# A decoder step on one core: another order of the last down projection and its norm, and sample states loaded three ahead

## The chip, the core and the metric

The kernel runs on one core of a Trainium2 chip. The metric is device time in microseconds, the median of several runs. The engines that matter are TensorE (PE, matmuls), VectorE (DVE), ScalarE (ACT), GpSimd (POOL, here mostly an issuer of DMAs) and SyncE (SP, an issuer of DMAs). Each engine works through its own instructions in order and waits on semaphores for the others.

## The reference, cut to what matters

One layer of a hybrid decoder for 512 prompt tokens and 8 samples with one token each: a half-step SwiGLU feed-forward network, a mixer (pooling and a state space model), a second feed-forward network, and a last RMS norm. The change touches the second feed-forward network, the last norm, and the new states of the samples.

```python
h = h + 0.5 * _swiglu(_rms_norm(h, ffn1_norm), ...)      # D_MODEL 1024, FFN_DIM 2816
h = h + mixer(_rms_norm(h, mix_norm))
h = h + 0.5 * _swiglu(_rms_norm(h, ffn2_norm), ...)
y = _rms_norm(h, final_norm)
# new state of one sample, per head: decay * old state + (dt * x) outer B
h_new = exp(dt * A) * h0 + (dt * x)[:, None] * B[None, :]
```

## The kernel before, in words

The features lie on the 128 partitions and the 520 tokens (512 and 8) along the free dimension, in two halves of 260 (`HALVES`, `HB`). `h` holds 8 feature tiles of 520 tokens. Weights are float32; each is split into a rounded part (`whi`, cast by ACT, L107) and a rest (`wlo`, DVE, L108), and each product is three matmuls (`mm3`, L117 to L119).

The second feed-forward network works in three chunks of 8, 8 and 6 of its 22 hidden tiles. For each chunk, gate and up products are computed (PSUM tiles `A` and `BE`), and then the down projection adds the chunk to `h`. The weights of `w2gu` and `w2d` come in loads issued by SP into two raw pairs of buffers; a load is issued when DVE has read the pair that it overwrites.

**Down stages of the first two chunks** (`down`, L350): for each of 8 output tiles `d`, the weights are loaded and split, PE runs 48 matmuls into `dn`, and DVE adds the result to `h` (`td`, L367, then L371). Into these two stages the new states of the samples are woven: the generator `new_states` (L806) yields 16 steps, one for each sample and head group, and `STATES` (L37) says how many are taken ahead of each output tile. A step works on one tile `hs` of 128x4x128: POOL issues the loads of the row `br` (broadcast to all partitions) and of the old state `hs`; ACT scales `br` into a tile `so`, four times; DVE multiplies `hs` by the decay and adds `so`, four times; POOL issues the store `out_nss`. The loads run two steps ahead, in three buffers. All these DMAs stand in POOL's one queue of instructions, a load behind the store whose buffer it needs.

**Last chunk** (`down_by_half`, L392): all first halves of the tokens (b = 0) come first, then all second halves (b = 1), so that the norm of the first half runs beside the second half's matmuls. The accumulators `dh` are banks of 512 floats: two neighbouring output tiles share one tile of two banks (`BE`), others take single banks (`A`). Except for what is pinned with `keep_in_program_order`, a scheduler that simulates times orders the instructions at build time; in the program that it makes, PE takes up the output tiles out of their order and in pieces (2, 0, 3, 4, 6, 7 among others). `done` (L419) scales the accumulator (`th`, L422), adds it to `h` (L424) and calls `after2`, which sums the squares (`sumsq`, L141) into `last` and multiplies by the gain into `hg`.

**Norm** (`finish`, L540): one matmul with ones sums the squares over partitions (`psl`, L543; for the last output tile a second one, L545), ACT takes the square root, and DVE, in two quarters of 130 tokens, takes the reciprocal, multiplies four feature tiles at a time, and SP stores each piece of 4 tiles by 130 tokens.

Of the kernel before, what the change touches and what calls it, by code (L numbers as in the profile page):

```python
# [9 lines left out]
F32 = mybir.dt.float32  # L10
F32R = mybir.dt.float32r
AF = mybir.ActivationFunctionType
ALU = mybir.AluOpType
# [3 lines left out]
P = 128  # L17
D = 1024
# [3 lines left out]
HB = NT // 2  # L22
HALVES = (slice(0, HB), slice(HB, NT))
KD = D // P
# [9 lines left out]
CHUNKS = (8, 8, 6)  # L34
NG = 9
ON_ACT = 4
STATES = (0, 1, 1, 1, 2, 1, 1, 1)  # L37

CONV_PLAN = (
    "b0 b1 d0 b2 b3 x0 x1 v0 d1 x2 x3 d2 X0 p0 y0 c0 A0 p1 x4 m0 x5 B0 c1 p2 m1 A1 x6 c2 p3 A2 B1 x7 "  # L40
# [22 lines left out]
def tile_trunk_step(ctx: ExitStack, tc: tile.TileContext, ins: dict, outs: dict):  # L63
    nc = tc.nc
# [7 lines left out]
    tmp = ctx.enter_context(tc.tile_pool(name="tmp", bufs=3, side="right"))  # L72
    dr = ctx.enter_context(tc.tile_pool(name="dr", bufs=1, space=DRAM))
    ps = [None]
# [6 lines left out]
    h = vx[:, NVEC:].rearrange("p (d t) -> p d t", d=KD)  # L81
# [4 lines left out]
    ones = cst.tile([P, P], F32, tag="ones", name="ones")  # L86
    nc.vector.memset(ones, 1.0)
    eps = cst.tile([P, 1], F32, tag="eps", name="eps")
# [24 lines left out]
        nc.sync.dma_start(out=raw, in_=src)  # L113
        return split(raw, n, name, wp, 3, ("whi", "wlo"))

    def mm3(ps, whi, wlo, xhi, xlo, start, stop, **kw):
        nc.tensor.matmul(ps, whi, xhi, start=start, stop=False, **kw)  # L117
        nc.tensor.matmul(ps, whi, xlo, start=False, stop=False, **kw)  # L118
        nc.tensor.matmul(ps, wlo, xhi, start=False, stop=stop, **kw)  # L119

    def ws(w, k, m=P):
        return w[:, k * m : (k + 1) * m]
# [18 lines left out]
    def sumsq(acc, d, hs, name):  # L141
        n = hs.stop - hs.start
        if d == 0:
            nc.scalar.activation(out=acc[:, hs], in_=h[:, d, hs], func=AF.Square)
        else:
            sq = tmp.tile([P, HB], F32, tag="ta", name=f"sq_{name}_{d}")
            nc.scalar.activation(out=sq[:, :n], in_=h[:, d, hs], func=AF.Square)
            nc.vector.tensor_tensor(out=acc[:, hs], in0=acc[:, hs], in1=sq[:, :n], op=ALU.add)
# [47 lines left out]
    class Ffn:  # L196
# [195 lines left out]
        def down_by_half(self, c, lo, after, wd):  # L392
            n = KF - lo
            banks, units = {}, []
            for d in range(KD):
                src, name = ins[f"w{self.i}d"][d, :, lo * P :], f"{self.i}d{d}_{c}"
                raw = raw_tile(name)[:, : n * P]
                nc.sync.dma_start(out=raw, in_=src)
                if d < 4:
                    home = (wp, 3, ("whi", "wlo")) if d < 2 else (self.wx, 2, ("shi", "slo"))  # L400
                    units.append(split(raw, n * P, name, *home))
                    continue
                hi, lw = (wd.tile([P, n * P], F32R, tag=t, bufs=KD - 4, name=f"{t}_{name}") for t in ("dhi", "dlo"))
                nc.scalar.copy(hi, raw)
                nc.vector.tensor_tensor(out=lw, in0=raw, in1=hi.bitcast(F32), op=ALU.subtract)
                units.append((hi, lw))

            def part(d, b, ks):
                if (d, b) not in banks and d % 4 < 2:
                    t = ps[0].tile([P, 2, 512], F32, tag="BE", bufs=2, name=f"dh{self.i}_{d}{b}")  # L410
                    banks[d, b], banks[d + 1, b] = t[:, 0], t[:, 1]
                elif (d, b) not in banks:
                    banks[d, b] = ps[0].tile([P, 512], F32, tag="A", bufs=2, name=f"dh{self.i}_{d}{b}")
                wh, wl = units[d]
                for k in ks:
                    g = self.g[lo + k]
                    mm3(banks[d, b][:, :HB], ws(wh, k), ws(wl, k), g[:, 0, b], g[:, 1, b], k == 0, k == n - 1)

            def done(d, b):  # L419
                hs = HALVES[b]  # L420
                t = self.wx.tile([P, 2, HB], F32, tag="tg", bufs=2, name=f"th{self.i}_{d}{b}")[:, 0]
                nc.vector.scalar_tensor_tensor(out=t, in0=banks[d, b][:, :HB], scalar=-0.5, in1=self.nx[3][:, hs],  # L422
                                               op0=ALU.mult, op1=ALU.mult)
                nc.vector.tensor_tensor(out=h[:, d, hs], in0=t, in1=h[:, d, hs], op=ALU.add)  # L424
                after(d, b, hs)

            for d in range(3):
                part(d, 0, range(n - 1))
            for b in range(2):
                for d in range(KD):  # L430
                    part(d, b, range(n - 1, n) if b == 0 and d < 3 else range(n))
                    done(d, b)
# [10 lines left out]
    for j in range(KD // 2):  # L443
        for d in (j, j + KD // 2):
            q = slice(NVEC + d * NT if d else 0, NVEC + (d + 1) * NT)
# [70 lines left out]
    last = act.tile([P, NT], F32, tag="acc", name="acc_last")  # L516
    res = []

    def before2():
# [3 lines left out]
        res.append(f2["hg"].tile([P, NT], F32, tag="rl", name="r_last"))  # L523
        return f2["hg"]

    def after2(d, b, hs):
        hg = res[0]
        if (d, b) == (KD - 1, 1):
            sq = tmp.tile([P, HB], F32, tag="ta", name="sq_last")
            nc.scalar.activation(out=sq, in_=h[:, d, hs], func=AF.Square)  # L530
            nc.vector.tensor_scalar(out=hg[:, d, hs], in0=h[:, d, hs], scalar1=v("final_norm", d), scalar2=None,
                                    op0=ALU.mult)
            finish(1, sq)
            return
        sumsq(last, d, hs, f"l{d}{b}")
        nc.scalar.activation(out=hg[:, d, hs], in_=h[:, d, hs], func=AF.Copy, scale=v("final_norm", d))
        if (d, b) == (KD - 1, 0):
            finish(0)

    def finish(b, sq=None):  # L540
        hs, hg, rl = HALVES[b], *res
        ps = bank(f"psl{b}")
        nc.tensor.matmul(ps[:, :HB], ones, last[:, hs], start=True, stop=sq is None)  # L543
        if sq is not None:
            nc.tensor.matmul(ps[:, :HB], ones, sq, start=False, stop=True)  # L545
        nc.scalar.activation(out=rl[:, hs], in_=ps[:, :HB], func=AF.Sqrt, bias=eps, scale=1.0 / D)
        cuts = (hs.start, hs.start + HB // 2, hs.stop)
        for t in (slice(cuts[0], cuts[1]), slice(cuts[1], cuts[2])):
            n = t.stop - t.start
            tc.keep_in_program_order(nc.vector.reciprocal(out=rl[:, t], in_=rl[:, t]))  # L550
            for q in (slice(0, 4), slice(4, KD)):
                nc.vector.tensor_tensor(out=hg[:, q, t], in0=hg[:, q, t],
                                        in1=rl[:, t].unsqueeze(1).to_broadcast([P, 4, n]), op=ALU.mult)
                nc.sync.dma_start(out=outs["y"][:, q, t], in_=hg[:, q, t])

    f2["ffn"].rest(before2, after2)
    for p in (ps[0], f2["st"], g2, f2["hg"], f2["wx"]):
# [3 lines left out]
def mixer(tc, ins, outs, e):  # L561
    nc = tc.nc
    cst, act, wp, tmp, dr, pool = (e[x] for x in ("cst", "act", "wp", "tmp", "dr", "pool"))
    ones = e["ones"]
    bank, load_unit, mm3, ws, v, rstd, rstds, vec, h, nx2, raw_tile, open_f2, fin, fill = (
        e[x] for x in ("bank", "load_unit", "mm3", "ws", "v", "rstd", "rstds", "vec", "h", "nx2", "raw_tile",
                       "open_f2", "fin", "fill"))
    xh, xl, _, r = nx2[0]
# [183 lines left out]
    sdec = cst.tile([P, NX, NS], F32, tag="sdec", name="sdec")  # L752
# [52 lines left out]

    def new_states(wx):  # L806
        def load(b, g):
            br = wx.tile([P, P], F32, tag="sb", bufs=3, name=f"br{b}{g}")
            tc.keep_in_program_order(nc.gpsimd.dma_start(out=br, in_=rows_bc(b, 0, g)))
            hs = wx.tile([P, 4, P], F32, tag="sh", bufs=3, name=f"hs{b}{g}")  # L810
            tc.keep_in_program_order(nc.gpsimd.dma_start(out=hs, in_=ins["state_ssm"][:, b, 4 * g : 4 * g + 4]))
            return br, hs

        todo = [(b, g) for g in range(2) for b in range(NS)]
        ahead = [load(*todo[0]), load(*todo[1])]
        for i, (b, g) in enumerate(todo):
            yield
            br, hs = ahead.pop(0)
            if i + 2 < len(todo):
                ahead.append(load(*todo[i + 2]))  # L820
            o = wx.tile([P, 4, P], F32, tag="so", bufs=2, name=f"so{b}{g}")
            for q in range(4):
                j = 4 * g + q
                tc.keep_in_program_order(
                    nc.scalar.activation(out=o[:, q], in_=br, func=AF.Copy, scale=sxdt[:, j, b : b + 1]))
                tc.keep_in_program_order(
                    nc.vector.scalar_tensor_tensor(out=hs[:, q], in0=hs[:, q], scalar=sdec[:, j, b : b + 1],
                                                   in1=o[:, q], op0=ALU.mult, op1=ALU.add))
            tc.keep_in_program_order(nc.gpsimd.dma_start(out=outs["nss"][:, b, 4 * g : 4 * g + 4], in_=hs))
        yield  # L830

# [268 lines left out]
```

## Time and profile before

| | |
|---|---|
| median of 3 runs | 1002.59 us (1002.44 to 1002.99) |
| profiled execution | 1003.51 us, its span 1000.5 us |
| granted TensorE clock | 0.994 (mean) |
| busy: PE, DVE, ACT, POOL | 97%, 81%, 53%, 9% of the span |
| chain that ended last | PE 88%, DVE 6%, ACT 2%, POOL 2% |
| stores of `y` (8) | 260 KB each, median 3.5 us from issue to landing |
| state loads and stores (16 each) | 256 KB each, median 3.6 and 3.1 us |

Times within the profile are microseconds from the start of the span. In a row of the timeline the first number is the start, the second the time until the end of the last of the instructions in the row, and in brackets stands how long the engine was idle before it and for whom it waited. "x4" counts instructions. A DMA's row on POOL or SP is the time to issue it, not the transfer.

### The profile page before, as it was taken

The numbers are of one execution on the slowest core, as the hardware profiler recorded it, in microseconds if no ns is written. First come the engines' busy times: TensorE is split into PE (matmuls) and PEld (weight loads), VectorE is DVE, ScalarE is ACT, GpSimd is POOL, SyncE is SP. The second block draws the span as 40 slices with busy tenths as digits, with TensorE's granted clock in tenths as the row PEclk, the third lists the DMA queues.
The fourth block names the chain that finished last, engine by engine and source line by source line (L and its number), as shares of the span: only waits on it lengthen the run. The fifth ranks groups of instructions, "written<-read, shape, count | busy, mean of one in ns | idle before, by whom it ended". The sixth has DMA issues, their size and how long they took to land.

```text
span 1000.5 us, 19362 instructions
## 1 busy us (share of the span) xinstructions
PE 971.7 (97%) x7850; PEld 951.4 (95%) x7850; DVE 806.9 (81%) x1408; ACT 528.7 (53%) x881; POOL 87.8 (9%) x157
## 2 busy tenths in 40 slices
PE   7999999999999999999999999999999999999994
PEld 6899999999999999999899998899999999999993
DVE  7999657996569688788979987999957999668865
ACT  7566414664145455684845235666743666436552
POOL 0000000000000000167312000100012000120000
PEclk9999999999999999999999999999999999999997
DMA  6333232323223223263334421423346333452213
GB/s 194 112 126 114 98 101 73 124 88 124 85 85 106 85 104 117 87 216 105 107 133 122 146 90 54 124 94 118 127 137 187 120 127 118 124 195 96 95 33 85
DMA packets 44072, 114.44 MB, mean 114 GB/s; under 512 B 6408, under 2 KB 15560, under 8 KB 43984
## 3 DMA queue, kind: packets, MB, share of 16 engines
q1 hardware_dynamic: 40912, 103.78, 30.7%
q0 software_dynamic: 3072, 9.44, 3.5%
q8 instruction: 61, 1.00, 0.4%
q14 instruction: 27, 0.22, 0.1%
HBM read 105.86 MB, written 7.34 MB: 113 GB/s over the span
## 4 chain that ended last, share of the span: by engine, by line
PE 88%; DVE 6%; ACT 2%; POOL 2%; issue 1%; DMA 0%; SPq 0%; DVEq 0%; ACTq 0%
PE A L119 8%; PE A L117 8%; PE A L118 8%; PE dn L117 7%; PE dn L119 7%; PE dn L118 7%; PE BE L117 6%; PE BE L119 6%; PE BE L118 6%; PE P L232 4%; PE wo L117 2%; PE wo L118 2%; PE wo L119 2%; PE inz L117 2%; PE inz L119 2%; PE inz L118 2%
## 5 line engine op out<-in xcount | busy, mean ns | idle before, releaser
L117 PE MATMUL dn<-g,whi_1d 128*128 128x260 f32 x352 | 99.3, 283 | 0.2 <-DVE td L367 0.2
L118 PE MATMUL dn<-g,whi_1d 128*128 128x260 f32 x352 | 99.5, 283 | 0.0
L119 PE MATMUL dn<-g,wlo_1d 128*128 128x260 f32 x352 | 99.4, 283 | 0.0
L367 DVE SCALAR_TENSOR_TENSOR td<-dn,r_f 128x520 f32<-128x520 f32 x40 | 27.9, 699 | 73.2 <-PE dn L119 73.2
L119 PE MATMUL dn<-g,wlo_2d 128*128 128x260 f32 x256 | 72.4, 283 | 0.0
L118 PE MATMUL dn<-g,whi_2d 128*128 128x260 f32 x256 | 72.3, 282 | 0.0
L117 PE MATMUL dn<-g,whi_2d 128*128 128x260 f32 x256 | 72.3, 282 | 0.0
L117 PEld LDWEIGHTS dn<-g,whi_1d 128*128 128x128 f32 x352 | 66.1, 188 | 0.4 <-DVE td L367 0.4
L118 PEld LDWEIGHTS dn<-g,whi_1d 128*128 128x128 f32 x352 | 66.3, 188 | 0.0
L119 PEld LDWEIGHTS dn<-g,wlo_1d 128*128 128x128 f32 x352 | 66.2, 188 | 0.0
L297 ACT COPY ac<-A 128x260 f32<-128x260 f32 x123 | 45.6, 374 | 29.3 <-PE A L119 28.0
L107 ACT CAST whi_1d<-raw_1d 128x1024 fp32r<-128x1024 f32 (+1 forms) x24 | 23.4, 980 | 67.0 <-PE dn L118 54.2
L260 DVE TENSOR_TENSOR s<-raw 128x1024 f32<-128x1024 f32 x41 | 50.0, 1220 | 3.9 <-DMA raw<-in_w2gu 3.9
L232 PE MATMUL P<-xg_f,raw 128*128 128x260 f32 x192 | 45.1, 392 | 6.2 <-DMA raw<-in_w1gu 5.4
L232 PEld LDWEIGHTS P<-xg_f,raw 128*128 128x128 f32 x192 | 36.9, 195 | 12.1 <-ACT xg_f L179 5.4
L117 PEld LDWEIGHTS dn<-g,whi_2d 128*128 128x128 f32 x256 | 48.3, 189 | 0.0
L118 PEld LDWEIGHTS dn<-g,whi_2d 128*128 128x128 f32 x256 | 48.2, 188 | 0.0
L119 PEld LDWEIGHTS dn<-g,wlo_2d 128*128 128x128 f32 x256 | 48.2, 188 | 0.0
L118 PE MATMUL wo<-catg,whi_wo 128*128 128x260 f32 x128 | 36.4, 285 | 1.3 <-DVE catg L957 1.3
L117 PE MATMUL wo<-catg,whi_wo 128*128 128x260 f32 x128 | 37.3, 292 | 0.3 <-DVE h L926 0.3
L117 PE MATMUL inz<-xh_mx,whi_inz 128*128 128x260 f32 x128 | 36.8, 287 | 0.1
L117 PE MATMUL inx<-xh_mx,whi_inx 128*128 128x260 f32 x128 | 36.4, 284 | 0.0
(1340 smaller groups left out, 3924.1 us busy)
## 6 DMA issues: line engine op xcount, KB each, us to landing
raw<-in_w2gu SPq DMA_DIRECT2D x44, 512.0 KB, 4.5
raw<-in_w1gu SPq DMA_DIRECT2D x42, 512.0 KB, 4.4
raw_1d<-in_w1d SPq DMA_DIRECT2D x16, 512.0 KB, 4.4
raw_2d<-in_w2d SPq DMA_DIRECT2D x16, 512.0 KB, 4.6
raw_wo<-in_w_out SPq DMA_DIRECT2D x12, 512.0 KB, 5.0
ab<-scr_acs SPq DMA_DIRECT2D x8, 512.0 KB, 4.8
h<-in_state_ssm SPq DMA_DIRECT2D x16, 256.0 KB, 4.2
raw_inz<-in_w_in SPq DMA_DIRECT2D x8, 512.0 KB, 3.9
```

What stands on the lines that cost most here:

```text
L107: nc.scalar.copy(h, src)
L117: nc.tensor.matmul(ps, whi, xhi, start=start, stop=False, **kw)
L118: nc.tensor.matmul(ps, whi, xlo, start=False, stop=False, **kw)
L119: nc.tensor.matmul(ps, wlo, xhi, start=False, stop=stop, **kw)
L232: nc.tensor.matmul(self.banks[f, u][b][:, :HB], ws(self.raw[f][:, u], j + 4 * q), xg[:, slot[q]], start=j == q == 0, stop=j == 3 and q == ...
L260: nc.vector.tensor_tensor(out=s1, in0=diag, in1=up0, op=ALU.add)
L297: nc.scalar.copy(keep, out[:, :HB])
L367: nc.vector.scalar_tensor_tensor(out=t, in0=banks[d][:, :, :HB], scalar=-0.5, in1=self.nx[3].rearrange("p (b t) -> p b t", b=2), op0=ALU.mult,
```

## The change

The changed kernel does two things.

In the last chunk each output tile gets an accumulator bank of its own; the first matmul of each second-half tile (except output tile 1's) is pinned to the program order. The norm of the first half is started by the first tile of the second half and is spread over the tiles that follow: one reciprocal or one product with its store per tile. Products and stores cover 2 feature tiles by 260 tokens. In the second half the squares of the last two output tiles are kept apart and go to `psl` as matmuls of their own, three in all, and the square root is taken in two quarters.

For the states, loads run three steps ahead in four buffers. ACT multiplies the loaded state by the decay in place, and DVE adds the scaled row; the tile `so` is gone. `STATES` takes its first step ahead of output tile 2 and two steps ahead of tiles 3 and 5.

```diff
-STATES = (0, 1, 1, 1, 2, 1, 1, 1)
+STATES = (0, 0, 1, 2, 1, 2, 1, 1)
...
-    def mm3(ps, whi, wlo, xhi, xlo, start, stop, **kw):
-        nc.tensor.matmul(ps, whi, xhi, start=start, stop=False, **kw)
+    def mm3(ps, whi, wlo, xhi, xlo, start, stop, pin=False, **kw):
+        first = nc.tensor.matmul(ps, whi, xhi, start=start, stop=False, **kw)
+        if pin:
+            tc.keep_in_program_order(first)
...
-                if (d, b) not in banks and d % 4 < 2:
-                    t = ps[0].tile([P, 2, 512], F32, tag="BE", bufs=2, name=f"dh{self.i}_{d}{b}")
-                    banks[d, b], banks[d + 1, b] = t[:, 0], t[:, 1]
-                elif (d, b) not in banks:
-                    banks[d, b] = ps[0].tile([P, 512], F32, tag="A", bufs=2, name=f"dh{self.i}_{d}{b}")
+                if (d, b) not in banks:
+                    if b == 0 and d in (2, 3):
+                        banks[d, b] = bank(f"dh{self.i}_{d}{b}")
+                    elif d % 2:
+                        banks[d, b] = ps[0].tile([P, 512], F32, tag="A", bufs=2, name=f"dh{self.i}_{d}{b}")
+                    else:
+                        t = ps[0].tile([P, 2, 512], F32, tag="BE", bufs=2, name=f"dh{self.i}_{d}{b}")
+                        banks[d, b] = t[:, 0]
...
-                    mm3(banks[d, b][:, :HB], ws(wh, k), ws(wl, k), g[:, 0, b], g[:, 1, b], k == 0, k == n - 1)
+                    mm3(banks[d, b][:, :HB], ws(wh, k), ws(wl, k), g[:, 0, b], g[:, 1, b], k == 0, k == n - 1,
+                        pin=b == 1 and k == 0 and d != 1)
...
     def after2(d, b, hs):
         hg = res[0]
+        if (d, b) == (0, 1):
+            finish(0, [last[:, HALVES[0]]])
+        elif b and todo:
+            todo.pop(0)()
+        if b and d >= KD - 2:
+            late.append(tmp.tile([P, HB], F32, tag="ta", name=f"sq_last{d}"))
+            nc.scalar.activation(out=late[-1], in_=h[:, d, hs], func=AF.Square)
+        else:
+            sumsq(last, d, hs, f"l{d}{b}")
         if (d, b) == (KD - 1, 1):
...
-            finish(1, sq)
+            finish(1, [last[:, hs], *late])
+            while todo:
+                todo.pop(0)()
             return
...
+    def finish(b, sqs):
         hs, hg, rl = HALVES[b], *res
         ps = bank(f"psl{b}")
+        for k, sq in enumerate(sqs):
+            nc.tensor.matmul(ps[:, :HB], ones, sq, start=k == 0, stop=k == len(sqs) - 1)
+        cuts = (0, HB // 2, HB)
+        quarters = [slice(cuts[i], cuts[i + 1]) for i in range(2)]
+        for q in quarters:
+            nc.scalar.activation(out=rl[:, hs][:, q], in_=ps[:, q], func=AF.Sqrt, bias=eps, scale=1.0 / D)
+
+        def inverse(q):
+            tc.keep_in_program_order(nc.vector.reciprocal(out=rl[:, hs][:, q], in_=rl[:, hs][:, q]))
+
+        def out(d):
+            tc.keep_in_program_order(
+                nc.vector.tensor_tensor(out=hg[:, d : d + 2, hs], in0=hg[:, d : d + 2, hs],
+                                        in1=rl[:, hs].unsqueeze(1).to_broadcast([P, 2, HB]), op=ALU.mult))
+            nc.sync.dma_start(out=outs["y"][:, d : d + 2, hs], in_=hg[:, d : d + 2, hs])
+
+        todo.extend([lambda q=q: inverse(q) for q in quarters])
+        todo.extend([lambda d=d: out(d) for d in range(0, KD, 2)])
...
-            br = wx.tile([P, P], F32, tag="sb", bufs=3, name=f"br{b}{g}")
+            br = wx.tile([P, P], F32, tag="sb", bufs=4, name=f"br{b}{g}")
...
-            hs = wx.tile([P, 4, P], F32, tag="sh", bufs=3, name=f"hs{b}{g}")
+            hs = wx.tile([P, 4, P], F32, tag="sh", bufs=4, name=f"hs{b}{g}")
...
-        ahead = [load(*todo[0]), load(*todo[1])]
+        ahead = [load(*t) for t in todo[:3]]
...
-            if i + 2 < len(todo):
-                ahead.append(load(*todo[i + 2]))
-            o = wx.tile([P, 4, P], F32, tag="so", bufs=2, name=f"so{b}{g}")
+            if i + 3 < len(todo):
+                ahead.append(load(*todo[i + 3]))
...
-                    nc.scalar.activation(out=o[:, q], in_=br, func=AF.Copy, scale=sxdt[:, j, b : b + 1]))
+                    nc.scalar.activation(out=hs[:, q], in_=hs[:, q], func=AF.Copy, scale=sdec[:, j, b : b + 1]))
...
-                    nc.vector.scalar_tensor_tensor(out=hs[:, q], in0=hs[:, q], scalar=sdec[:, j, b : b + 1],
-                                                   in1=o[:, q], op0=ALU.mult, op1=ALU.add))
+                    nc.vector.scalar_tensor_tensor(out=hs[:, q], in0=br, scalar=sxdt[:, j, b : b + 1], in1=hs[:, q],
+                                                   op0=ALU.mult, op1=ALU.add))
```

## The prediction

> **What bounds the kernel now.** I read the page first: TensorE is busy 97% of the span, and 88% of the chain that ended last is PE. So an edit is worth something only where PE stops, or after PE has ended. From PE's start times in the timeline from 640 us on (pitch 0.12 us per 128x260 matmul) I then listed each place where the next matmul came late. Between 657.5 and 958.7 us there is none above 0.07 us. The whole stage in which the sample states are written lies in there, so its waits are covered today. Losses begin at 958.67 us, with the last matmuls. The chain in order of time shows them (start, us, engine, tile, line):
>
> ```profile
> 958.99 0.44 DVE th L422
> 959.47 0.39 PE dh L117
> ...
> 979.91 0.35 DVE th L422
> 980.30 0.39 PE dh L117
> 984.91 0.77 DVE th L422 x2
> ...
> 987.28 0.44 DVE acc_last L148
> 987.76 1.14 PE psl L543 x2
> 988.90 0.88 PE psl L545 x2
> 989.81 0.49 ACT r_last L546
> ```
>
> Twice PE waits for `th` to read a PSUM bank that it shares with another accumulator, and after the last matmul (start 984.60) a row of DVE and ACT steps runs before the sum of squares `psl`. PE's own timeline gives these waits, in brackets:
>
> ```profile
> 959.47 0.39 PE L117 MATMUL dh<-g,whi_2d 128*128 128x260 f32 x1 [0.52 <-DVE th L422]
> 980.30 0.39 PE L117 MATMUL dh<-g,dhi_2d 128*128 128x260 f32 x1 [0.73 <-DVE th L422]
> 987.76 1.14 PE L543 MATMUL psl<-acc_last,ones 128*128 128x260 f32 x2 [2.89 <-DVE acc_last L148]
> ```
>
> Behind that, the stores. In stretches of 1 us (engines, clock, DMA share, GB/s), the first-half store at 978 and the last ones:
>
> ```profile
> 978.00:979.00 1.00, 1.00 (x11) 1.00 (x10) 1.00 (x4) 0.55 (x2) 0.00 (x0) 1.00 1.01 290
> 993.00:994.00 1.00, 0.00 (x0) 0.00 (x0) 0.96 (x2) 0.00 (x0) 0.00 (x0) 0.50 0.97 279
> 997.00:998.00 1.00, 0.00 (x0) 0.00 (x0) 0.00 (x0) 0.00 (x0) 0.00 (x0) 0.50 0.96 166
> ```
>
> 1.06 MB takes from 993.0 to 998.1 us, and the clock has fallen to 0.50 while PE stood. For the states, POOL's timeline of the first of two down stages is what matters:
>
> ```profile
> 747.70 0.54 POOL L829 DMA_DIRECT2D out_nss<-hs  x1 [2.60 <-DVE hs L827]
> 748.24 0.53 POOL L809 DMA_DIRECT2D br<-scr_bc  x1
> 752.24 0.54 POOL L811 DMA_DIRECT2D hs<-in_state_ssm  x1 [3.47 <-DMA out_nss<-hs]
> 753.93 0.54 POOL L829 DMA_DIRECT2D out_nss<-hs  x1 [1.16 <-DVE hs L827]
> 756.53 0.54 POOL L811 DMA_DIRECT2D hs<-in_state_ssm  x1 [1.53 <-DMA out_nss<-hs]
> ```
>
> One queue holds loads and stores: a load waits until an earlier store has landed, and everything behind it waits too.
>
> The profiled execution took 1003.51 us, its span 1000.5, so 3.0 us lie around it; the median of the runs is 1002.59, 0.92 less. I sum against 1003.51 and take the difference to the median. 0.2% is 2.0 us, about what a measurement can tell from no change.
>
> **The end: accumulators and order.** No matmul of the last down stage is added or lost (288 before and after). In the changed order PE finishes one output tile after another, and each tile has a bank of its own. A bank is wanted again at the earliest 23 matmuls (2.8 us) after its last one; `th` starts 0.31 us after a last matmul and ends within 0.46 us, also where six tiles finish together (it then reads the fifth 3.1 us after the first, and that bank is wanted after 36 matmuls, 4.3 us). So both waits go: 0.80 less one pitch is 0.68, plus 0.11 for the slow matmul behind it, and 0.88 plus 0.11. **Minus 1.8 us.** The first-half norm is spread over the second half: per tile DVE then does `th` 0.46, `h` 0.34, a reciprocal 0.88 or a product 0.65, and a sum 0.34: 1.8 to 2.0 us against 18 x 0.12 = 2.16 of PE. That cover is thin (0.15 us); were it gone, each tile would add its excess. The in-order reciprocal waits for two square roots behind `psl0`; `psl0` starts 1.0 us before them (973.25 to 973.89 for the matmul, then 0.4), and the next `th` is due 2.4 us after `psl0` starts, so it is in time. The first four stores now leave during the second half, on an otherwise idle SP queue.
>
> **The end: after the last matmul.** Before, from its start to the root: 984.60 to 989.81 = 5.21 us, because two tiles ended together and both sums came late. After, the sum of tiles 0 to 5 and the square of tile 6 are ready, so two of the three `psl1` matmuls run at once (0.55 each, ended by 1.3). The path is `th` 0.31 later, `h` 0.46 later, square 0.51 later (985.60 to 986.11), its 0.47, and one matmul to root 0.64 (the row at 973.25): 2.39. **Minus 2.8 us**, or 2.3 if that matmul runs slow as at 988.69 (1.12). I take the fast row, as PE idles under 0.6 us instead of 2.9.
>
> **The end: norm and stores.** From root start, before: last byte at 998.1, 8.3 us. After: the 130-wide root is not in the trace; between nothing and the 260-wide 0.48 I take 0.40 to the reciprocal. Then 0.88 + 1.00 for two reciprocals, 0.70 for the first product, 0.06: first store at 3.04 (before 2.27), the fourth at 5.0 (5.06). Traffic begins 0.95 later (992.08 to 993.0). 1.06 MB in rows of 1040 B, which the trace lacks: as slow as now, 5.05 us, ends at 9.05 (0.75 worse); at half the packets for half the time, the last store bounds it at 6.8 (1.5 better). I take 290 GB/s, the nearest row of the same tensor: 3.7 us, end at 7.7. **Minus 0.6 us.** The Trainium skill, DMA: Bandwidth & Descriptors, Specifications, says that transfers from 512 B up reach line rate; by it, rows of 520 B are already as fast as 1040 B and this term is 0.75 worse. The trace speaks against it: 166 to 290 GB/s with 520 B rows, 389 to 426 in the saturated microseconds of the 4 KB rows of `w2gu` (761 and 887 us).
>
> The end gives 1.8 + 2.8 + 0.6 = **5.2 us** (3.4 to 6.1).
>
> **The states.** 64 ACT scalings of 128x128 (388 ns) and 64 DVE steps (346 ns) stay as many and as long; only tiles and order change. A fourth pair of loads leaves at the start of the stage (around 647 us); the next weights were loaded by then and the following load is issued at 653.77, so it costs nothing, at most 1 us without that cover. What matters: ACT now scales the loaded state itself, so it waits for `hs`, and DVE for `br` too. In the new order ACT does state 4, the cast for down tile 5, states 5 and 6, and only then the cast `whi` of down tile 6; so this cast, the DVE rest `wlo` behind it, and PE's tile 6 wait for state 6. Its load: store 1 is issued where a store is issued now (747.70), the next load again at 752.24, store 2 at 752.78 (its result is done at 748.45); it lands after 2.3 to 4.3, say 2.5: load 6 at 755.3. The weight load of 1 MB is issued at 754.95, when `wlo` of tile 5 is done. State loads beside such a load took 6.6 (756.53, 0.7 after it) and 4.7 (768.08, 0.7 ahead of it); I take 5.7: 761.0. Then four scalings 1.18, cast 1.05, rest 1.22 and hand-overs 0.15: 764.6. PE's third matmul of tile 6 is due at 763.44 + 0.24 = 763.68. **Stall 0.9 us**, between 0 and 3.5.
>
> In the second stage the same rows are 874.44, 879.54, 880.08, 882.9; the weight load comes 1.3 us ahead of load 14, the nearest row (883.63) took 6.0, and as the weights leave 1 us sooner I take 5.5: 888.4, done 892.0, due 890.42. **Stall 1.6 us**, 0 to 4.3. ACT's waits of 3.16 and 3.52 us for `br` go, but PE never felt them: worth nothing.
>
> Sum: -5.2 + 2.5 = -2.7 us: 1000.8 against 1003.51, so **999.9** against the median.
>
> **Rivals.** *No stall:* loads 6 and 14 land as undisturbed ones do (2.9 to 3.1 us), at 758.4 and 886.0, before 760.1 and 886.8 from where PE waits. For it: load 6 is issued nearly together with the weights. Against it: 6.0 and 6.6 in the nearest rows. It gives -5.2: 997.4. The Trainium skill, DMA: Bandwidth & Descriptors, SWDGE vs HWDGE vs iDMA, says that each engine goes round-robin between the queues, which would give the smaller state load its share early, this case; the trace does not agree: the state load issued at 883.63, 1.05 us behind the weights, took 6.0.
>
> *Slower:* the states take over as bound. Its place is the cast of down tile 6 behind state 6 on ACT, twice. If the stores 2 and 10 also meet traffic (4.3 us as at 747.70, about 5 as at 874.44), the loads leave at 757.1 and 885.1 and land at 763.7 and 891.1: stalls of 3.6 and 4.3. It decides where both stalls exceed 5.2 together, landing after about 762.7 and 889.4. It gives -5.2 + 7.9 = +2.7: 1005.3. Against it: stores without weight traffic took 2.3 to 3.
>
> *The end gives less:* stores no faster (0.75 worse) and a slow last matmul (2.3): 1.8 + 2.3 - 0.75 = 3.4, less 2.5 of stall: -0.9, 1001.7, no change. For it: the store rate fell while four were in flight.
>
> **How the numbers follow.** Main case 0.52, no stall 0.25, slower 0.10, weak end 0.13. The likeliest gives 999.9. The main case reaches from 998.6 to 1001.1 (stalls 1.2 to 3.7); about 0.42 of its 0.52 is below 1000.6, with the 0.25 of no stall 0.67 faster; 0.10 + 0.13 within 0.2%; 0.10 slower. The range goes from no stall with the better store bound, 996.5, to 1002.9, which leaves out most of the slower case and a little below.
>
> **What would show it.** Right: no PE gap between 958 and the end of the `dh` matmuls; 2.3 to 2.9 us from the last of them to the second root; about 7.7 us from root to last byte; PE waiting for ACT or DVE at the start of `dn` tile 6 in both stages, behind a scaling that waits for DMA `hs`. Wrong: no such wait (then 997), waits over 2.6 us each, or PE waits in the second half for a bank that the reciprocal on DVE holds up.

## The result, and the profile after

The changed kernel takes 1008.08 us (median of 4 runs, 1007.68 to 1009.3) where the kernel before takes 1002.79 us (1002.44 to 1003.19): ratio 1.0055, 95% interval 1.004 to 1.007. It is slower by 5.3 us; the forecast was 999.9, with a range up to 1002.9. The profiled execution took 1008.25 us with a span of 1006.5, 6.0 longer than before.

Two groups of matmuls of the down stages on the page (busy us, mean ns, then the idle time before them and who ended it), first before, then after; line 119 has become line 121:

```profile
L117 PE MATMUL dn<-g,whi_2d 128*128 128x260 f32 x256 | 72.3, 282 | 0.0
L119 PE MATMUL dn<-g,wlo_2d 128*128 128x260 f32 x256 | 72.4, 283 | 0.0
```

```profile
L117 PE MATMUL dn<-g,whi_2d 128*128 128x260 f32 x256 | 74.3, 290 | 5.5 <-ACT whi_2d L107 5.5
L121 PE MATMUL dn<-g,wlo_2d 128*128 128x260 f32 x256 | 74.4, 291 | 1.2 <-DVE wlo_2d L108 1.2
```

PE is as busy as before, in share (97%). But the matmuls of the down stages now wait 5.5 us for ACT's cast and 1.2 us for DVE's rest (both 0 before), the mean matmul takes 290 ns instead of 282, and the page's row of the granted clock, in 40 slices, has an 8 in place of a 9 at the second stage (slice 36, from 880 us). I listed PE's start times again against the pitch of 0.12 us: 5.0 us are lost between 763 and 772, 6.5 us between 895 and 905, none elsewhere between 658 and the end. PE's timeline at the first place, start first:

```profile
763.42 0.28 PE L121 MATMUL dn<-g,wlo_2d 128*128 128x260 f32 x1
765.89 0.39 PE L117 MATMUL dn<-g,whi_2d 128*128 128x260 f32 x1 [2.19 <-ACT whi_2d L107]
766.12 0.28 PE L120 MATMUL dn<-g,whi_2d 128*128 128x260 f32 x1
767.15 0.39 PE L121 MATMUL dn<-g,wlo_2d 128*128 128x260 f32 x1 [0.75 <-DVE wlo_2d L108]
```

That is down tile 6. Over the pitch, PE is 2.35 and 0.91 us late, 3.3 together. Behind ACT's cast, in the timelines of ACT, DVE, POOL and SP (SPq is SP's issue of DMAs):

```profile
763.63 1.28 ACT L844 ACTIVATE hs<-hs,sdec 128x128 f32<-128x128 f32 x4 [6.60 <-issue]
764.81 1.97 ACT L107 CAST whi_2d<-raw_2d 128x1024 fp32r<-128x1024 f32 x2
...
765.87 1.23 DVE L108 TENSOR_TENSOR wlo_2d<-raw_2d,whi_2d 128x1024 fp32r<-128x1024 f32 x1 [4.37 <-ACT whi_2d L107]
```

```profile
753.06 0.54 POOL L848 DMA_DIRECT2D out_nss<-hs  x1
...
756.57 0.54 POOL L831 DMA_DIRECT2D hs<-in_state_ssm  x1 [2.44 <-DMA out_nss<-hs]
...
755.23 0.33 SPq L255 DMA_DIRECT2D raw<-in_w2gu  x1
```

ACT stands idle for 6.6 us ahead of the scaling of state 6 (763.63); the row calls it "issue", but the load of that state, issued at 756.57, took 7.0 us to land, near 763.6. The casts of tiles 6 and 7 follow 1.2 us later; that of tile 6 could have run from 757.9 on, when PE had finished with tile 4 and so left it a buffer. In the kernel before it ran there:

```profile
756.84 1.05 ACT L107 CAST whi_2d<-raw_2d 128x1024 fp32r<-128x1024 f32 x1 [1.84 <-issue]
```

Load 6 left behind store 2 (753.06, 3.2 us to land), 1.3 us after the first half of the weights. At the second place the same chain shows: load 14 issued at 889.30, landed after 7.2 us, scaling at 896.52, cast at 897.71, PE 3.49 and 0.76 us late.

3.3 and 4.25 us of waiting are not 5.0 and 6.5. The rest is the clock. Stretches of the first place, cut where the granted clock changes (columns: length, PE, PEld, DVE, ACT and POOL busy, clock, DMA share, GB/s):

```profile
764.40:767.80 3.40, 1.16 (x7) 0.95 (x8) 1.93 (x2) 2.48 (x5) 1.60 (x3) 1.00 0.50 158
767.80:771.20 3.40, 3.40 (x18) 3.40 (x18) 3.40 (x6) 1.19 (x4) 1.60 (x3) 0.50 0.44 121
771.20:774.60 3.40, 3.40 (x30) 3.40 (x30) 1.73 (x6) 0.21 (x1) 1.60 (x3) 1.00 0.68 113
```

PE, back at work since 765.89, starts 18 matmuls in a stretch of 3.4 us where it starts 30 in the next. At the second place the clock is 0.50 for 6.8 us (897.5 to 904.3). That is 1.7 and 2.3 us on top of the waits, which the prediction has no term for.

The end did what it was to do. The timeline there (line numbers of the changed kernel):

```profile
994.40 0.28 PE L121 MATMUL dh<-g,dlo_2d 128*128 128x260 f32 x1
...
996.92 0.63 ACT L562 ACTIVATE r_last<-psl,eps 128x130 f32<-128x130 f32 x2 [0.80 <-PE psl L558]
```

From the start of the last `dh` matmul to the root it is 2.52 us (before 5.21), to the end of the span 12.1 (before 984.60 to 1000.5, 15.9). The stores of 1040 B rows run at 340, 354 and 312 GB/s from 1001 to 1004, where those of 520 B fell from 279 to 166:

```profile
1001.00:1002.00 1.00, 0.00 (x0) 0.00 (x0) 0.68 (x2) 0.00 (x0) 0.00 (x0) 0.50 1.03 340
...
1003.00:1004.00 1.00, 0.00 (x0) 0.00 (x0) 0.00 (x0) 0.00 (x0) 0.00 (x0) 0.50 0.92 312
```

With the two waits for `th` gone (1.8), the end gives 3.8 + 1.8 = 5.6 us. Balance of the two spans: -5.6 + 5.0 + 6.5 = +5.9 against 6.0 measured.

### The profile page after: what moved, and what is told of

Read it like the earlier page. It is cut to its first block, busy times and chain, and to the rows that moved or that the text cites. A ratio compares the mean times of both kernels' runs of the same rounds, so it can differ in the third digit from the quotient of the medians.

```text
span 1006.5 us, 19375 instructions
## 1 busy us (share of the span) xinstructions
PE 976.7 (97%) x7852; PEld 955.9 (95%) x7852; DVE 807.1 (80%) x1407; ACT 528.6 (53%) x883; POOL 85.6 (9%) x157
## 4 chain that ended last, share of the span: by engine, by line
PE 85%; DVE 8%; ACT 2%; issue 2%; POOL 2%; DMA 0%; SPq 0%; DVEq 0%; ACTq 0%
PE A L121 8%; PE A L117 8%; PE A L120 8%; PE dn L121 7%; PE dn L117 7%; PE dn L120 7%; PE BE L117 6%; PE BE L121 6%; PE BE L120 6%; PE P L234 2%; PE wo L117 2%; PE wo L120 2%; PE wo L121 2%; PE inz L117 2%; PE inz L121 2%
## 5 line engine op out<-in xcount | busy, mean ns | idle before, releaser
L117 PE MATMUL dn<-g,whi_2d 128*128 128x260 f32 x256 | 74.3, 290 | 5.5 <-ACT whi_2d L107 5.5
L120 PE MATMUL dn<-g,whi_2d 128*128 128x260 f32 x256 | 74.1, 289 | 0.0
L117 PEld LDWEIGHTS dn<-g,whi_2d 128*128 128x128 f32 x256 | 50.1, 196 | 5.9 <-ACT whi_2d L107 5.9
L120 PEld LDWEIGHTS dn<-g,whi_2d 128*128 128x128 f32 x256 | 50.0, 195 | 0.0
```

What stands on the lines that cost most here:

```text
L117: first = nc.tensor.matmul(ps, whi, xhi, start=start, stop=False, **kw)
```

## The experiments

The theory, called "late load" below: loads 6 and 14 land with the weights; ACT scales in order, so the cast of down tile 6 stands behind them; PE stops; its clock falls. The rivals are named with each run. The kernel before was timed again beside each set of runs: 1004.95 us (1002.31 to 1005.78) beside the first four, 1003.52 (1002.31 to 1006.17) beside the next four. So compare the ratios rather than the medians.

**Each half alone.** The first run takes the end from the changed kernel and the states from the kernel before, the second the other way round.

```diff
 # end alone: the changed kernel with
-STATES = (0, 0, 1, 2, 1, 2, 1, 1)
+STATES = (0, 1, 1, 1, 2, 1, 1, 1)
 # and new_states() of the kernel before; states alone: the kernel before with
-STATES = (0, 1, 1, 1, 2, 1, 1, 1)
+STATES = (0, 0, 1, 2, 1, 2, 1, 1)
 # and new_states() of the changed kernel
```

> The kernel before with the reworked end alone: states loaded two ahead and scaled into their own buffer, steps (0, 1, 1, 1, 2, 1, 1, 1). Theory 'late load' (loads 6 and 14 land with the weights, the cast of down tile 6 sits behind them on ACT, PE stops, and its clock falls): the whole loss comes with the states, so the end gives what the traces show of it, 3.8 after the last matmul and 1.8 of PE waits: 997.2 us (996.7 to 997.8), no PE gap between 640 and the end but the 3.5 us in the first 20 us of that stretch. Rival 'the end costs' (the new order or the steps of the spread norm hold PE up or delay the next pass): 1003 or more. Rival 'the parts depend on each other' (the gaps of the states' stages come from the end's pinned order): gaps at 763 and 895 here as well, about 1008.

> The kernel before with the states' part alone: loaded three ahead, decayed in place, steps (0, 0, 1, 2, 1, 2, 1, 1); the end as before. Theory 'late load': plus 4.9 and 6.5 us of lost PE time, and 1002.8 + 11.4 = 1014.2 us (1013 to 1015.5). Rival 'the end costs': 1002.8, no new gap. Rival 'the parts depend on each other': between the two, and a sum of the effects of the two single parts that is not the +5.3 of both together.

End alone: 997.94 us, ratio 0.9933 (0.9914 to 0.9952). States alone: 1014.49 us, ratio 1.0095 (1.0079 to 1.0111). So the end is a gain and the states are the whole loss, 7.9 to 11.2 us by the interval. The PE timeline of the states alone has the two places again, 4.9 and 5.8 us lost, with the old end behind them:

```profile
767.23 0.39 PE L117 MATMUL dn<-g,whi_2d 128*128 128x260 f32 x1 [2.23 <-ACT whi_2d L107]
...
899.71 0.39 PE L117 MATMUL dn<-g,whi_2d 128*128 128x260 f32 x1 [3.02 <-ACT whi_2d L107]
```

One thing was not expected: the end alone showed a wait of 1.2 us for DVE's rest of down tile 7 at 896.7, which the kernel before does not have. It is taken up in the last run.

**Old steps.** One line of the changed kernel is put back, so that the scaling of state 6 comes behind the cast of tile 6.

```diff
-STATES = (0, 0, 1, 2, 1, 2, 1, 1)
+STATES = (0, 1, 1, 1, 2, 1, 1, 1)
```

> The changed kernel with one line put back: the steps per down tile are (0, 1, 1, 1, 2, 1, 1, 1) again, so that state 6 belongs to tile 7 and its scaling stands behind the cast of tile 6; loads three ahead and decay in place stay. Theory 'late load': load 6 may land as late as it likes, no cast that PE is waiting for stands behind it; load 7 is the next that could, and it is one store later, in front of the casts of tile 7: no gap, 997.3 us, at most 1 us more. Rival 'in place' (an ACT scaling that waits for a load is enough by itself, wherever it stands, or in-place decay costs more on ACT and DVE): gaps of over 2 us in both stages stay, 1004 to 1009.

997.38 us, ratio 0.9927 (0.9909 to 0.9946). ACT's timeline is the answer:

```profile
756.77 1.06 ACT L107 CAST whi_2d<-raw_2d 128x1024 fp32r<-128x1024 f32 x1
...
762.95 1.28 ACT L844 ACTIVATE hs<-hs,sdec 128x128 f32<-128x128 f32 x4 [4.48 <-DMA hs<-in_state_ssm]
764.14 1.04 ACT L107 CAST whi_2d<-raw_2d 128x1024 fp32r<-128x1024 f32 x1
```

The load of state 6 is as late as ever (issued 756.54, 6.3 us, landed 762.9), and ACT waits 4.5 us for it. But the cast of tile 6 is at 756.77, and what stands behind the wait is the cast of tile 7, in time. PE has no gap in either stage. Being late costs nothing where nothing urgent stands behind it; decay in place costs nothing by itself.

**New steps, old roles.** The new steps with the states as before (rows scaled by ACT into `so`, two ahead), and the reworked end.

```diff
 # new_states() of the kernel before in the changed kernel:
-                    nc.scalar.activation(out=hs[:, q], in_=hs[:, q], func=AF.Copy, scale=sdec[:, j, b : b + 1]))
+                    nc.scalar.activation(out=o[:, q], in_=br, func=AF.Copy, scale=sxdt[:, j, b : b + 1]))
```

> The reworked end, the new steps (0, 0, 1, 2, 1, 2, 1, 1), but the states as before: ACT scales the broadcast row into a buffer of its own, DVE decays the loaded state, two loaded ahead. ACT waits only for the rows, which are issued ahead of the states and are small; DVE waits for the loaded state and stands ahead of the rest of tile 6. Theory 'late load': the loads of states 5 and 6 now wait for stores 2 and 3 and land among the weights, and DVE's rests of tile 6 stand behind state 5: a gap of 1 to 5 us in each stage, 999 to 1007, and PE waits for DVE and not for ACT's cast. Rival 'in place' (it takes ACT's wait for the state): no gap, 997.2. Rival 'too much work in two steps' (the two states between tiles 5 and 6 are 2 x 1.55 us of ACT and 2 x 1.4 of DVE, too much for the time of a tile, whatever lands): a gap of some 1 us with ACT and DVE busy without a wait throughout.

1000.27 us, ratio 0.9954 (0.9938 to 0.9971): 2.3 us behind the end alone, and its timeline loses 0.6 us in the first stage and 1.6 us in the second:

```profile
766.09 0.39 PE L121 MATMUL dn<-g,wlo_2d 128*128 128x260 f32 x1 [0.35 <-DVE wlo_2d L108]
...
894.41 0.39 PE L121 MATMUL dn<-g,wlo_2d 128*128 128x260 f32 x1 [1.30 <-DVE wlo_2d L108]
```

The wait is for DVE, and DVE's timeline shows what stands ahead of that rest: a state whose load, issued at 758.66 behind the weights, landed at 763.6.

```profile
763.76 1.14 DVE L847 SCALAR_TENSOR_TENSOR hs<-hs,sdec,so 128x128 f32<-128x128 f32 x4 [1.51 <-DMA hs<-in_state_ssm]
764.82 1.22 DVE L108 TENSOR_TENSOR wlo_2d<-raw_2d,whi_2d 128x1024 fp32r<-128x1024 f32 x1
```

DVE stood 1.5 us for the load here and 2.4 us in the second stage, more than PE lost, so the work of two steps is not too much for it. The late load is at work here too, through DVE instead of ACT and for a smaller price; both stops (0.5 and 1.5 us) leave the clock at 1.00. The "in place" rival expected no gap at all.

**Four ahead.** Now only the load is moved earlier; steps, roles and the order on ACT stay as in the change.

```diff
-            hs = wx.tile([P, 4, P], F32, tag="sh", bufs=4, name=f"hs{b}{g}")
+            hs = wx.tile([P, 4, P], F32, tag="sh", bufs=5, name=f"hs{b}{g}")
...
+            if i + 4 < len(todo):
+                ahead.append(load(*todo[i + 4]))
```

> The changed kernel, with the sample states loaded four ahead instead of three (five buffers for them; the broadcast rows stay three ahead). Steps, roles and the order on ACT and DVE stay as in the change. Load 6 now waits for store 1 and not for store 2, so it should leave where load 5 leaves in the change, near 752.5, 2.7 us ahead of the weights, and land near 755 to 756; load 14 likewise near 880. Theory 'late load': the cast of down tile 6 still stands behind the scaling of state 6, but finds it done: no gap at 763 and 895, 997.3 us (996.5 to 998.5), and the clock stays at 1.00 there. Rival 'too much work in two steps' or 'in place': the order is the same, so the gaps stay, 1005 or more. A middle result, 999 to 1003, would say that load 6 leaves early but still lands among the weights.

997.13 us (996.49 to 1000.14), ratio 0.994 (0.9921 to 0.9958), no gap in either stage. Load 6 leaves 2.7 us ahead of the weights and lands after 3.0 us, and ACT scales it at 758.37; the cast of tile 6 then waits only for PE:

```profile
755.23 0.54 POOL L834 DMA_DIRECT2D hs<-in_state_ssm  x1 [3.47 <-DMA out_nss<-hs]
...
758.37 1.28 ACT L850 ACTIVATE hs<-hs,sdec 128x128 f32<-128x128 f32 x4 [1.48 <-DMA hs<-in_state_ssm]
760.74 1.05 ACT L107 CAST whi_2d<-raw_2d 128x1024 fp32r<-128x1024 f32 x1 [1.09 <-PE dn L120]
```

With the same work in the same order, only the time of the load differs: this rules out that two steps ahead of a tile are too much.

**Stores on SP.** The other way to let load 6 leave early: POOL no longer holds store 2 behind a load that waits.

```diff
-            tc.keep_in_program_order(nc.gpsimd.dma_start(out=outs["nss"][:, b, 4 * g : 4 * g + 4], in_=hs))
+            tc.keep_in_program_order(nc.sync.dma_start(out=outs["nss"][:, b, 4 * g : 4 * g + 4], in_=hs))
```

> The changed kernel, with the stores of the sample states issued by SP instead of POOL; everything else as in the change. POOL then no longer holds a store behind a load that waits: store 2 leaves when its result is done (near 748.5) and not at 753.06, lands near 752, and load 6 leaves near 752.5 and lands near 755 to 756. Theory 'late load': no gap, 997.3 us, as long as SP's stores do not hold up its weight loads. Against it, within the theory: a store that waits for DVE in SP's queue holds the weights behind it (at most 2 us, which the prefetch should cover), and stores land no faster among the weights. Rivals: as for four ahead, the gaps stay.

997.2 us (7 runs, 996.3 to 1001.79), ratio 0.9942 (0.9923 to 0.9962), no gap. Load 6 left at 753.43, 1.7 us ahead of the weights, and took 4.3 us: 757.8. The weights landed at 764.2 instead of 762.9; nobody waited for them.

**Casts first.** Here the load stays late, and the cast is taken out from behind it.

```diff
-                    units[d] = load_unit(ins[f"w{self.i}d"][d, :, lo * P : hi * P], n * P, f"{self.i}d{d}_{c}")
+                    with tc.high_priority() if self.i == 2 else nullcontext():
+                        units[d] = load_unit(ins[f"w{self.i}d"][d, :, lo * P : hi * P], n * P, f"{self.i}d{d}_{c}")
```

> The changed kernel, with the casts of the down tiles of the second multilayer perceptron given a higher priority, so that ACT does the cast of tile 6 before it scales state 6, and DVE the rest of tile 6 early too. Loads and stores leave as in the change: load 6 near 756.6, and it lands near 763.5 among the weights. Theory 'late load': it is late as before, but no work that PE waits for stands behind it: no gap above 0.5 us, 997.3 us (996.5 to 998.5). Rival 'late weights' (not the order on ACT, but the transfers themselves, which share the queues, hold up what PE needs): the gaps stay, 1005 or more.

997.1 us, ratio 0.9932 (0.9915 to 0.9948), no gap in either down stage. Load 6 left later still (757.73) and landed at 762.6, 1.0 us earlier than in the change and far too late for a cast behind it; the cast ran at 758.12, ahead of the scaling:

```profile
758.12 1.03 ACT L107 CAST whi_2d<-raw_2d 128x1024 fp32r<-128x1024 f32 x1
762.65 1.28 ACT L845 ACTIVATE hs<-hs,sdec 128x128 f32<-128x128 f32 x4 [3.50 <-DVE hs L847]
```

So both links are needed, the late load and the cast behind it: breaking either gives all of the loss back.

**The clock by itself.** Extra DVE work that changes no value holds PE at the same place in the kernel before, without any late load.

```diff
+                    if self.i == 2 and d == 6:
+                        wl = units[d][1]
+                        for _ in range((4, 7)[c]):
+                            nc.vector.tensor_tensor(out=wl, in0=wl.bitcast(F32), in1=wl.bitcast(F32), op=ALU.max)
```

> The kernel before with extra DVE work ahead of the use of down tile 6: its rest is rewritten with the maximum of itself and itself, four times in the first stage and seven times in the second (1.13 to 1.22 us each, and other DVE work between them). It leaves the values as they are and has no extra load, and holds PE for an estimated 1.5 to 3 us in the first stage and 5 to 8 us in the second. Theory 'late load' with its part on the clock: PE that stands for over 2 us is granted half the clock some 2 us after it begins again, for about 3 us, which costs 1.4 to 2 us on top of the wait; so in the second stage rows of 0.50 and a pitch of 0.215 us must follow the wait, without any late load; in the first stage only if the wait is over about 2 us, and then the time lost is the wait plus 1.4 to 2 us. Rival 'the pitch is slow since operands come late' (weight casts that are just in time, DMA traffic): after these waits the pitch is 0.12 at once, and only the wait is lost.

One run, 1023.41 us. PE stood 4.2 us in the first stage, more than the estimate, and 5.2 in the second (later waits follow from the moved work), and the clock was 0.50 for 6.8 us in each, not for about 3 (768.9 to 775.8, 905.5 to 912.3). At 0.50 the matmuls start 0.22 us apart, so the rival is out. No late load is needed for the fall of the clock. A run with two and five rewrites followed, for shorter stops.

> As the held rest, with two rewrites in the first stage and five in the second, for shorter waits. From the run with four and seven (PE stood 4.2 and 5.2 us there), less two rewrites of 1.2 us each: an estimated 1.8 and 2.8 us, and about 1 us more at the next matmul that waits for the rest. The clock's part of the theory: windows of about 3.3 us, by what the rows of 0.50 in the change (3.2 us and 6.6 us) and with four rewrites (6.8 us) show; a wait that leaves PE working for less than half of such a window costs the next window at half clock. So I expect 0.50 for about 3.3 us after the wait of 2.8, and after that of 1.8 either nothing or one such window. If both show 1.00 throughout, the wait has to be over 2.8 us, and the gap of 2.4 us in the change's first stage is not enough by itself.

One run, 1013.71 us. My estimate of the waits was wrong: PE stood 3.25 and 4.1 us, not 1.8 and 2.8, since other DVE work slid between. So the shortest stop in these two runs is longer than that of the change. But they show the windows. Cut at the changes of the clock and 3.4 us back from them (columns as above):

```profile
764.10:767.50 3.40, 0.39 (x3) 0.39 (x4) 3.40 (x5) 2.21 (x5) 1.60 (x3) 1.00 0.50 154
767.50:770.90 3.40, 3.40 (x18) 3.40 (x18) 3.40 (x8) 0.00 (x0) 0.54 (x1) 0.50 0.40 110
...
893.80:897.20 3.40, 1.82 (x16) 1.61 (x14) 2.52 (x3) 1.04 (x4) 1.00 (x2) 1.00 0.21 83
897.20:900.60 3.40, 0.48 (x2) 0.30 (x2) 3.40 (x5) 1.17 (x2) 0.08 (x1) 1.00 0.50 157
```

A stretch with 0.39 or 0.48 us of PE work is followed by 3.4 us at 0.50 (the second of them from 900.6 to 904.0); one with 1.82 us is followed by full clock. In the change, 1.16 us (764.4 to 767.8, above) and 1.36 us (894.1 to 897.5) were followed by 0.50. So the limit lies between 1.36 and 1.82 us of work in 3.4.

Two things in the same traces say more. The changes of the clock within one trace lie whole multiples of 3.413 us apart: in the change at 767.81, 771.22, 897.51 and 904.34 (0, 1, 38 and 40 of them), in the run with four and seven rewrites 84 and 124 of them after a first one at 482.22. So the stretches seem to be cut by a beat of their own, and not by the stop of PE. And work as the profile counts it does not give a sharp limit: 1.66 us was followed by full clock in one stretch of the run with four and seven rewrites (898.65 to 902.06) and by 0.50 in one of "Four ahead" (583.12 to 586.53, in the mixer), and 1.77 us by 0.50 in the former (478.8 to 482.2).

How long a stop may be before it costs a window depends on where it falls: 4.1 us cost one window here, 3.5 us cost two in the change.

**Is the states' part worth anything once it is harmless?** Three kernels from above again, five rounds on one chip.

> The end alone once more, beside the two ways of keeping the states' part, in more rounds, to see whether the states' part is worth anything once it no longer stops PE. Theory: PE never felt ACT's waits for the broadcast rows, so nothing: all three kernels within 0.1% of each other, near 997.2 us where the kernel before takes 1002.8. Rival: the end alone keeps a wait for DVE of about 1 us at down tile 7 of the second stage (seen once, 1.2 us), and then it is about 0.1% behind.

> The changed kernel with the old steps once more: within 0.1% of the end alone by the theory; 1 us ahead by the rival.

> The changed kernel with the casts of the down tiles first once more: within 0.1% of the end alone by the theory; 1 us ahead by the rival.

The kernel before took 1002.6 us there (1001.92 to 1003.51). End alone: 996.44, ratio 0.9939 (0.9925 to 0.9952). Old steps: 997.13, 0.9944 (0.9932 to 0.9957). Casts first: 996.67, 0.9941 (0.9929 to 0.9954). They can't be told apart. The end alone again has a wait for DVE, 0.7 us, at 896.1, and the old steps have none, but no time follows that can be measured. The version to keep is the end alone: it beats both kernels and has the least in it.

## Why the prediction was wrong

**The end: right.** PE waits -1.8 (forecast -1.8). Last matmul to root 2.52 us (forecast 2.39). Root to last byte some 7.1 us (7.7); the fast side of the store bound was the nearer one. Together -5.6 by the trace against -5.2; by the medians -7.0 in the first comparison (997.94 against 1004.95) and -6.2 in the last (996.44 against 1002.6). The thin cover of the spread norm held: no gap in the second half. The Trainium skill, DMA: Bandwidth & Descriptors, Specifications, gives 512 B as the least transfer for line rate, by which rows of 520 B would be as fast as 1040 B; that does not agree with 312 to 354 GB/s against 279 to 166 here. The shape of the pieces changed together with the row, and no run separates the two.

**The states: the place right, the size wrong, +11.5 instead of +2.5.** Of the 9.0 us between, 5.0 are waits and 4.0 the clock.

*The step that failed is the landing of load 6: it was to leave at 755.3, fly 5.7 us and land at 761.0.* It landed near 763.6, 2.6 later: 1.3 because store 2 left 0.3 later, took 3.2 instead of 2.5 us, and the load was issued 0.3 after it had landed; and 1.3 in the flight, which was 7.0 us; the wait became 3.3 us where 0.9 was forecast. For load 14 the forecast 888.4 moves to 893.4 with the 5.0 us lost before it, and it landed at 896.5, 3.1 later. The error under it was to take a duration from the issue of the load. The rows of before already held the better reading, in the landings of the weights beside them, which I had not looked up. State loads issued after the weights, and the second half of those weights (us):

| kernel, stage | load issued | weights landed | load landed |
|---|---|---|---|
| before, 1 | 756.53 | 762.5 | 763.1 |
| before, 2 | 883.63 | 889.0 | 889.6 |
| after, 1 | 756.57 | 762.9 | 763.6 |
| after, 2 | 889.30 | 895.8 | 896.5 |
| old steps, 1 | 756.54 | 762.2 | 762.9 |
| old roles, 1 | 758.66 | 763.0 | 763.6 |
| casts first, 1 | 757.73 | 761.9 | 762.6 |

Whenever such a load left, it landed 0.6 to 0.7 us after the weights; load 6 took 3.0 and 4.3 us in the two runs in which it left ahead of them. By that reading of before alone, with the weights at the issue times that I used, load 6 lands near 762 and the wait of the first stage is near 2 us (an estimate). The Trainium skill, DMA: Bandwidth & Descriptors, Queues, rings and completion order, says that the increment which reports a transfer lands only after every earlier write of the same DMA engine, across queues; the table agrees with that. But the DMA rows of the trace show more than a late report. From 757.5 to 760.0 the queue of SP moved 0.66 MB and the queue of POOL 0.00, though load 6 had been issued at 756.57; from 760.0 to 762.0 they moved 0.34 and 0.45. With old roles in the second stage it is 0.80 and 0.00 from 887.0 to 889.8, with the load issued at 886.14. So the bytes of the load came late, and an even share from the start is ruled out; why they came late stays open. Why the weights of the second stage took 8.8 us instead of 6.1 stays open; DMA engines were partly idle then.

*No term priced what follows a stop.* The prediction saw 0.50 in its own row after the last matmul ("the clock has fallen to 0.50 while PE stood") and did not carry it to its stalls: 1.7 and 2.3 us. The Trainium skill, TensorE: Matmul & The Clock Gate, Part 1, states half clock after one idle window of about 3.4 us, on a window that runs free. The 3.4 and 6.8 us at 0.50 agree in length, and the multiples of 3.413 us agree with a window that runs free; but windows with 1.16 and 1.36 us of work in them counted as idle too.

*The cover that was promised held:* the fourth load at the start of the stage cost nothing, and ACT's former waits for `br` were indeed worth nothing (the last three runs).

**The rivals.** "Slower" named the very place, and its waits of 3.6 and 4.3 us stand against 3.3 and 4.25. It got 0.10 because its condition was that stores 2 and 10 meet traffic; they did not (3.2 us), the flight of the loads was longer instead. That its landing of 763.7 is so near the measured one is therefore luck. What its 1005.3 lacks is in the main the clock. A wait whose cover was already negative in the main case, with an error of 2 us in a landing, deserved more than 0.10. "No stall" needed load 6 to land undisturbed: not beside the weights.

## What to carry to other kernels

When an engine that works in order waits for a DMA, list what stands behind the wait and who needs it; the cure is either an earlier load or an urgent instruction moved ahead, and here each gave back the whole loss. A small load that is issued behind a large one on another queue should be costed at the landing of the large one, as all seven in the table show, and not by its own duration. A stop of PE by 2.4 us or more cost more than itself here, another 1.5 to 2.6 us through the clock; stops of 0.5 to 1.5 us did not.

## What the runs showed of the hardware that was not expected

The halved clock comes in stretches of 3.4 us or a multiple (3.4, 6.8), and its start is not tied to that of PE: in the change it fell at 767.8, 1.9 us after PE had gone on, and at 897.5, 1.3 us before. 1.36 us of matmuls or less in the 3.4 us before was enough for it, 1.82 us was too much, and near 1.7 us both were seen. Loads issued on POOL's queue behind a 1 MB load on SP's moved 0.00 MB while that load moved 0.66 to 0.80 MB, and landed 0.6 to 0.7 us after it. And stores of 1040 B rows ran at 312 to 354 GB/s where those of 520 B rows had 166 to 290.
